# Layer boundary in an explicit order, dt weights side by side, head chains from k on, SSD in one cluster

## The chip, the cores and the metric

The kernel runs on one core of a Trainium2 chip. A core has a matrix engine (TensorE, PE in the profile), a vector engine (VectorE, DVE), an engine for pointwise functions (ScalarE, ACT), a general one (GpSimd, POOL) and an engine that here only issues transfers (SyncE, SP). Each works through its own queue of instructions in order, and semaphores hold an instruction back until what it needs is there. The metric is the device time of one execution in microseconds (us), as the median of several runs; lower is better.

## The reference

The input is one sequence of 256 frames of width 2048, ahead of which 16 learned meta tokens are set: 272 columns in the kernel (`T`). Two residual layers follow.

- Layer 0: `proj = h @ w_in` is cut into the operands of two kinds of attention, GLA (4 heads) and stick-breaking attention (8 heads of 128, operands sq, sk, sv and a gate sr). Both results, gated, are multiplied by `w_out`.
- Then `h = layer_norm(alpha * h + f)` over the 2048 features, and again behind layer 1.
- Layer 1: `z, xbc, dt = split(h @ w_in)`. `xbc` goes through a causal depthwise convolution of 4 taps and SiLU and is cut into x (8 groups of 8 heads of 64), B and C (one each per group). `dt` is one number per token and head, through softplus. The state-space scan (SSD) makes, for each head, `y[t] = sum over s <= t of exp(a[t] - a[s]) * (C[t] . B[s]) * dt[s] * x[s]` plus a skip term. y is gated by `silu(z)`, normalised per group and multiplied by a second `w_out`.

```python
for layer in range(DEPTH):          # 2
    f = even_mixer(h, ...) if layer % 2 == 0 else odd_mixer(h, ...)
    h = layer_norm(DEEPNORM_ALPHA * h + f, ln_g[layer], ln_b[layer])
return h[:, PREFIX:]                # the 256 frames
```

All of it is float32.

## The kernel before

**Products.** Activations and weights are both split into a high and a low part that TensorE takes at full rate, and a product is three matmuls: high by high, high weight by low activation, low weight by high activation (lines 165, 166, 167; `three`). The activations lie in `xhi` and `xlo` as 16 blocks of 128 features by 272 tokens (274 where two more columns carry the scale and the bias of the layer norm). 

**Weights.** They stream in as units of 1 MB (128 x 2048 values of `raw`, three buffers, SP's queue). Each unit is split in two halves: ScalarE writes the high part `whi` (line 146), VectorE the low part `wlo` = raw - whi (line 147; a few on GpSimd late in layer 1). `whi` and `wlo` have five buffers. While unit i is multiplied, `in_unit` splits unit i+1, one half ahead of each half of the matmuls, and loads unit i+2. A unit of an input projection is 48 matmuls, 24 for each half.

**Side tasks.** Everything else (heads, convolution, decay, normalisation) is written as Python generators that `tick` steps once at fixed places between matmuls. The order in which the kernel is written is not yet the order of the engines: a scheduler sorts each engine's instructions by its own estimate of when they can start, where no order is forced on it. In what follows "order" means the finished order of an engine's instructions.

**Head chains.** A stick-breaking head's chain (`mix_sb`) is pushed when its last operand v is there (`post_sv`). Its end writes `mixh` and `mixl`, which the last four units of layer 0 (`out0c`, numbers 4 to 7, the output projection of the last heads) read.

**The boundary.** Each `out0c` unit makes two blocks of 128 output features. `hacc` collects residual and output; when a block's sum is done (line 462), `stat0` writes the block's `xhi` and `xlo` (lines 815, 816: hacc scaled by the layer norm's g, not yet normalised) and adds to the sums `ssum` and `ssq` on GpSimd. `norm0` projects dt with 48 matmuls on 64 weight columns, sums `ssum` and `ssq` over the features with ones, and derives mean and 1/sigma per token, kept in two PSUM banks (`mean_p`, `rs_p`, the tiles z0 and z1 of the program). `first1` then multiplies the first six units of layer 1 (B, C, z0, x0, x1, x2) by the rows that are not yet normalised and puts mean and 1/sigma in afterwards (`fix`, lines 893 to 896). Meanwhile `normalize0` normalises `hacc` itself in 16 blocks: two steps on VectorE (lines 921, 922) and one on ScalarE (line 923). When that is through, `xhi` and `xlo` are rewritten (lines 914, 915) for the units from x3 on; `residual1` transposes `hacc` for the residual of layer 1 (lines 936, 937), and `dt_path` computes the decays. `units` goes on from the seventh unit.

**Behind a unit.** `post` takes a finished product out of PSUM: convolution (first tap on ScalarE, line 989; three more on VectorE, line 993), SiLU as Exp, Ln and Exp on ScalarE (lines 1001 to 1003). Four PSUM buffers `pj` hold products of units, two `po` all else.

**SSD.** Per group `mix_ssd` runs two clusters of fp32 matmuls for y, each for two pairs of heads (j and j+1): line 1159 (256 columns), line 1161 (144 columns), line 1163 (a corner of 16 columns on 16 rows). The two heads of a pair fill the two halves of PSUM's partitions. The operands of the corner are `mt` (16 rows, masked by C.B) and `xd2` (16 rows of dt * x). An fp32 matmul appears as two passes in the trace, each 12 matmuls of a cluster as 24 entries.

## Time and profile before

| | |
|---|---|
| runs of the kernel before | 1409.22, 1409.69, 1409.75 us; median 1409.69 |
| the profiled execution's own time | 1410.01 us |
| its span in the trace | 1408.3 us |
| granted TensorE clock, mean | 0.998 |
| matmuls / VectorE / ScalarE instructions | 10765 / 1613 / 1138 |
| last `out0c` matmul to the first matmul of x3 (the boundary) | 681.1 to 732.5 us |

The times of the steps below are those of the one profiled execution. In a timeline a row has the start, the length, the engine, the line of the code, the operation, what it writes and reads, the shape, and how many like it are put together; in brackets stands how long the engine was idle ahead of it and which instruction ended that. PE's matmuls overlap, so a matmul's length is longer than its step to the next. A group of instructions has busy time, mean length in ns, idle time of the engine ahead of it and what ended that.

### The profile page before, as it was taken

The numbers are of one execution on the slowest core, as the hardware profiler recorded it, in microseconds if no ns is written. First come the engines' busy times: TensorE is split into PE (matmuls) and PEld (weight loads), VectorE is DVE, ScalarE is ACT, GpSimd is POOL, SyncE is SP. The second block draws the span as 40 slices with busy tenths as digits, with TensorE's granted clock in tenths as the row PEclk, the third lists the DMA queues.
The fourth block names the chain that finished last, engine by engine and source line by source line (L and its number), as shares of the span: only waits on it lengthen the run. The fifth ranks groups of instructions, "written<-read, shape, count | busy, mean of one in ns | idle before, by whom it ended". The sixth has DMA issues, their size and how long they took to land.

```text
span 1408.3 us, 26132 instructions
## 1 busy us (share of the span) xinstructions
PE 1390.1 (99%) x10765; PEld 1332.7 (95%) x10765; DVE 1003.8 (71%) x1613; ACT 769.3 (55%) x1138; POOL 320.9 (23%) x285
## 2 busy tenths in 40 slices
PE   9999999999999999999999999999999999999996
PEld 8999999999999999999999999899898999989985
DVE  7857575575565675558799988776776868767587
ACT  6645454354345544555586866555555565555551
POOL 0000100100101100015301434343342432424323
PEclk9999999999999999999999999999999999999999
DMA  9544444545454445443446556555545455554551
GB/s 324 183 154 168 162 162 168 175 155 180 150 180 153 160 159 190 163 151 120 150 150 240 179 180 221 178 208 185 217 161 222 152 205 204 177 186 150 206 209 60
DMA packets 37718, 249.82 MB, mean 177 GB/s; under 512 B 4256, under 2 KB 6112, under 8 KB 9184
## 3 DMA queue, kind: packets, MB, share of 16 engines
q1 hardware_dynamic: 37168, 247.77, 50.3%
q8 instruction: 84, 1.38, 0.4%
q10 hardware_dynamic: 432, 0.39, 0.1%
q14 instruction: 34, 0.28, 0.1%
HBM read 245.94 MB, written 2.20 MB: 176 GB/s over the span
## 4 chain that ended last, share of the span: by engine, by line
PE 89%; DVE 6%; ACT 2%; issue 1%; DMA 1%; POOL 0%; ACTq 0%; SPq 0%; DVEq 0%; POOLq 0%
PE pj L165 23%; PE pj L166 23%; PE pj L167 23%; PE pj L476 4%; PE pj L478 4%; PE pj L477 4%; DVE wlo L147 2%; PE po L1159 1%; PE po L590 1%; ACT whi L146 1%; DVE xlo L816 1%; PE po L1161 1%; PE po L1163 0%; ACT hacc L923 0%; DMA ebc<-edr 0%
## 5 line engine op out<-in xcount | busy, mean ns | idle before, releaser
L165 PE MATMUL pj<-xhi,whi 128*128 128x272 f32 (+4 forms) x2560 | 734.1, 287 | 2.0 <-DVE fix L894 1.5
L166 PE MATMUL pj<-xlo,whi 128*128 128x272 f32 (+4 forms) x2560 | 731.7, 286 | 0.2 <-DVE xlo L318 0.2
L167 PE MATMUL pj<-xhi,wlo 128*128 128x272 f32 (+4 forms) x2560 | 730.3, 286 | 0.0
L147 DVE TENSOR_TENSOR wlo<-raw,whi 128x1024 fp32r<-128x1024 f32 (+2 forms) x405 | 507.0, 1256 | 254.4 <-ACT whi L146 253.1
L146 ACT ACTIVATE whi<-raw 128x1024 fp32r<-128x1024 f32 (+2 forms) x435 | 451.0, 1039 | 397.7 <-PE pj L166 335.3
L165 PEld LDWEIGHTS pj<-xhi,whi 128*128 128x128 f32 x2560 | 481.8, 188 | 4.7 <-DVE fix L894 1.9
L166 PEld LDWEIGHTS pj<-xlo,whi 128*128 128x128 f32 x2560 | 483.0, 189 | 1.8 <-issue 0.6
L167 PEld LDWEIGHTS pj<-xhi,wlo 128*128 128x128 f32 x2560 | 481.9, 188 | 0.3
L165 PE MATMUL pj<-mixh,whi 128*128 128x272 f32 x384 | 110.9, 290 | 1.0 <-ACT mixh L801 1.0
L167 PE MATMUL pj<-mixh,wlo 128*128 128x272 f32 x384 | 110.4, 288 | 0.0
L166 PE MATMUL pj<-mixl,whi 128*128 128x272 f32 x384 | 110.4, 288 | 0.0
L147 POOL TENSOR_TENSOR wlo<-raw,whi 128x1024 fp32r<-128x1024 f32 x30 | 75.4, 2513 | 132.5 <-ACT whi L146 132.4
L476 PE MATMUL pj<-whi,yh 128*128 128x512 f32 (+1 forms) x244 | 94.9, 391 | 0.0
L478 PE MATMUL pj<-whi,yl 128*128 128x512 f32 (+1 forms) x244 | 94.3, 387 | 0.0
L477 PE MATMUL pj<-wlo,yh 128*128 128x512 f32 (+1 forms) x244 | 94.2, 386 | 0.0
L248 POOL TENSOR_TENSOR gr<-gr,gsc 128x1088 f32<-128x1088 f32 x6 | 15.4, 2575 | 302.9 <-ACT gsc L247 302.9
L165 PEld LDWEIGHTS pj<-mixh,whi 128*128 128x128 f32 x384 | 72.2, 188 | 1.3 <-ACT mixh L801 1.1
L166 PEld LDWEIGHTS pj<-mixl,whi 128*128 128x128 f32 x384 | 72.3, 188 | 0.2
L167 PEld LDWEIGHTS pj<-mixh,wlo 128*128 128x128 f32 x384 | 72.3, 188 | 0.1
L485 DVE SCALAR_TENSOR_TENSOR acc<-pj,rr,acc 128x512 f32<-128x512 f32 (+1 forms) x65 | 47.2, 737 | 24.4 <-PE pj L478 24.3
L478 PEld LDWEIGHTS pj<-whi,yl 128*128 128x128 f32 x244 | 45.8, 188 | 9.2
L476 PEld LDWEIGHTS pj<-whi,yh 128*128 128x128 f32 x244 | 45.8, 188 | 9.0
(327 smaller groups left out, 1521.1 us busy)
## 6 DMA issues: line engine op xcount, KB each, us to landing
raw<-in_wts SPq DMA_DIRECT2D x212, 1024.0 KB, 4.8
ebc<-edr SPq DMA_DIRECT2D x8, 1664.0 KB, 6.5
raw<-in_wts SPq DMA_DIRECT2D x9, 256.0 KB, 6.2
hacc<-in_xT SPq DMA_DIRECT2D x7, 272.0 KB, 5.3
early<-in_wts SPq DMA_DIRECT2D x2, 512.0 KB, 6.9
lg<-in_lnr SPq DMA_DIRECT2D x1, 1024.0 KB, 4.7
lb<-in_lnr SPq DMA_DIRECT2D x1, 1024.0 KB, 4.6
out_h<-acc SPq DMA_DIRECT2D x2, 512.0 KB, 2.6
```

Of the source, the lines that this page charges most:

```text
L146: self.nc.scalar.activation(hi, src, AF.Copy)
L147: eng.tensor_tensor(lo, src, hi.bitcast(F32), op=ALU.subtract)
L165: mm(ps, whi, xhi, start=first, stop=False)
L166: mm(ps, whi, xlo, start=False, stop=False)
L167: mm(ps, wlo, xhi, start=False, stop=last)
L248: mul(c, c, e, op=ALU.mult)
L476: mm(ps, yh[:, kk, tt], hi[:, k, :], start=kk == 0, stop=False)
L477: mm(ps, yh[:, kk, tt], lo[:, k, :], start=False, stop=False)
L478: mm(ps, yl[:, kk, tt], hi[:, k, :], start=False, stop=kk == 3)
L485: self.nc.vector.scalar_tensor_tensor(a, ps, r[:, t : t + 1], a, op0=ALU.mult, op1=ALU.add)
L590: mm = lambda r, a, b, start=False, stop=False: self.nc.tensor.matmul(o[:, r], a, b, start=start, stop=stop, skip_group_check=True)
L816: vec.scalar_tensor_tensor(self.xlo[:, d, :T], x, g, self.xhi[:, d, :T].bitcast(F32), op0=ALU.mult, op1=ALU.subtract)
```

## The change

It has six parts.

1. **An explicit order.** `keep_order` ties every VectorE instruction to the one written ahead of it, and every ScalarE instruction likewise, from the start of the third `out0c` unit of the last four (number 6) to the end of `first1`. These are ties of order only, with no semaphore. What is written behind `first1` may still be put between.
2. **The normalisation in pairs.** `normalize0` takes two blocks in one VectorE step (544 columns instead of 272) and yields twice behind each pair. `first1` multiplies its first four units one after another, as before, and the last two in turns by halves, with the rewriting of `xhi` and `xlo` written in between. `residual1` and `dt_path` wait for `rows_done`.
3. **dt's weights side by side.** They are loaded and split two units earlier, high and low parts next to each other as 128 columns: two matmuls per block (by `xhi`, by `xlo`), 32 in all instead of 48. One fp32 matmul with `add2` (two identities under each other) adds the halves, after `rows_done`. The split of layer 1's second unit moves up into `norm0`.
4. **Head chains from k on.** `post_sk` pushes the chain, which waits for v only where v is used.
5. **SSD in one cluster.** The corners of the two pairs of heads of one PSUM bank become one matmul of 48 rows by 2 x 16 columns (rows 0 to 15 and 32 to 47 used, zeros else). `mt2` and `xd2` are cleared once and written by four small VectorE steps each per group. A group has one cluster of 20 matmuls, not two of 12.
6. Lines move: the three matmuls are lines 178 to 180 now, the split 159 and 160, `fix` 923 to 926, `normalize0` 983, 984 and 987, convolution 1058 and 1062, the rewriting 967 and 968, the sum into `hacc` 480, the transposes 1002 and 1003, SSD 1235 and 1241.

```diff
+    def keep_order(self, first):
+        ins = self.traced()
+        n0 = next(n for n in reversed(range(len(ins))) if ins[n] is first)
+        free = mybir.DependencyInfo(mybir.DependencyClass.NoSync, mybir.DependencyReason.DATA)
+        for eng in (mybir.EngineType.DVE, mybir.EngineType.Activation):
+            mine = [i for i in ins[n0:] if i.engine == eng]
+            for a, b in zip(mine, mine[1:]):
+                self.tc.add_manual_dep(b, a.name, free, reason="keep_order")
...
         if u[2] == 6:
-            self.dt_raw = self.lp.tile([P, 1024], F32, tag="gu", name="dtraw")
-            self.nc.sync.dma_start(self.dt_raw, self.wdt)
-        if u[2] == 7:
-            self.dt_parts = self.split(self.dt_raw, 1024)
+            self.first = self.traced()[-1]
+        if u[2] == 4:
+            self.dt_raw = self.lp.tile([P, 2, 8, 64], F32, tag="gu", name="dtraw")
+            self.nc.sync.dma_start(self.dt_raw.rearrange("p a k c -> p (a k c)"), self.wdt)
+        if u[2] == 5:
+            self.dt_parts = [self.lp.tile([P, 8, 2, 64], F32R, tag=n, name="dt" + n, bufs=2) for n in ("gvh", "gvl")]
+            for a, p in enumerate(self.dt_parts):
+                self.split_into(self.dt_raw[:, a], p[:, :, 0, :], p[:, :, 1, :], self.nc.vector)
...
     def post_sk(self, ps, h, j):
-        self.cur["k"] = self.sb_parts(ps, ("ke", "gk")[h % 2], 1.0)
+        k = self.sb_parts(ps, ("ke", "gk")[h % 2], 1.0)
+        v = self.cur["sv", h] = self.v_tiles(h)
+        self.mixers[4 + h // 4].append(self.push(self.mix_sb(h, self.cur["q"], k, v)))
...
-            self.in_kt(self.ps_dt[:64, :TG], hi[:, k, :], lo[:, k, :], k, 0, TG)
+            w = self.dt_parts[k // 8][:, k % 8].rearrange("p a c -> p (a c)")
+            mm(self.ps_dt[:, :TG], w, self.xhi[:, k, :], start=k == 0, stop=False)
+            mm(self.ps_dt[:, :TG], w, self.xlo[:, k, :], start=False, stop=k == KT - 1)
+        for h in range(2):
+            self.split_half(len(L0) + 1, h)
...
-        for n, u in enumerate(L1[:NFIRST]):
+        for n in range(NFIRST - 2):
...
+            if n == NFIRST - 3:
+                self.split_half(i + 2, 0)
...
+        for h in range(2):
+            for m, (n, ps) in enumerate(zip(ns, pss)):
+                if m == 0:
+                    self.load_unit(i + 2 + h)
+                else:
+                    self.split_half(i + 1 + h, 1 - h)
+                if (h, m) == (1, 1):
+                    self.split_half(i + 2, 1)
...
+                for k in range(8 * h, 8 * h + 8):
+                    self.in_kt(ps[:, : TG - t0], hv[:, k % 8, :], lv[:, k % 8, :], k, t0, TG)
+                    if m:
+                        act(self.xhi[:, k, :T], self.hacc[:, k, :], AF.Copy)
...
+                    if k % 4 == 3:
+                        self.tick()
+        for n, ps in zip(ns, pss):
+            self.post(L1[n], fix(ps, P, T0(n)))
+        self.rows_done = True
+        self.keep_order(self.first)
 
     def normalize0(self):
-        for k in range(KT):
-            h = self.hacc[:, k, :]
-            nc.vector.tensor_tensor(h, h, self.mean_p, op=ALU.subtract)
-            nc.vector.tensor_tensor(h, h, self.rs_p, op=ALU.mult)
-            nc.scalar.activation(h, h, AF.Identity, bias=self.col(C_LB, k), scale=self.col(C_LG, k))
-            if k % 2:
-                yield
+        two = lambda a: a.rearrange("p (o t) -> p o t", o=1).broadcast_to([P, 2, T])
+        for k in range(0, KT, 2):
+            h = self.hacc[:, k : k + 2, :]
+            nc.vector.tensor_tensor(h, h, two(self.mean_p), op=ALU.subtract)
+            nc.vector.tensor_tensor(h, h, two(self.rs_p), op=ALU.mult)
+            for kk in (k, k + 1):
+                a = self.hacc[:, kk, :]
+                nc.scalar.activation(a, a, AF.Identity, bias=self.col(C_LB, kk), scale=self.col(C_LG, kk))
+            yield
+            yield
...
+                for p, o in enumerate(os):
+                    for s, t0, c0, c1 in ((0, 0, 0, 256), (1, 112, 256, 400)):
+                        for jj in range(2):
+                            for i in range(2):
+                                h = 4 * p + 2 * jj + i
+                                mm(
+                                    o[i * 64 : (i + 1) * 64, jj, t0:S], xd[:, s, h * 64 : (h + 1) * 64], M[:, h, c0:c1],
```

Three places of the finished order show what moves. The first is VectorE at the start of layer 1. Before, from the fix of B on (`fix`, `uv`), the steps of the normalisation (L921, L922, on `hacc`) stand in blocks, with the splits (`wlo`, L147) of several units behind them:

```order
L921 TENSOR_TENSOR hacc<-hacc,z_64 128x272 x3
L894 SCALAR_TENSOR_TENSOR fix_8216<-dt_scr,uv_8215,pj_8134 128x272
L921 TENSOR_TENSOR hacc<-hacc,z_64 128x272 x8
L147 TENSOR_TENSOR wlo_8369<-raw_8226,whi_8368 128x1024
L895 TENSOR_TENSOR dt_scr<-dt_scr,z_65 64x272
L922 TENSOR_TENSOR hacc<-hacc,z_65 128x272 x8
L895 TENSOR_TENSOR fix_8216<-fix_8216,z_65 128x272
L922 TENSOR_TENSOR hacc<-hacc,z_65 128x272 x8
L893 COPY uv_8309<-pj_8228 128x2
L147 TENSOR_TENSOR wlo_8420<-raw_8319,whi_8419 128x1024
L147 TENSOR_TENSOR wlo_8460<-raw_8319,whi_8459 128x1024
L147 TENSOR_TENSOR wlo_8516<-raw_8416,whi_8515 128x1024
```

Now, from the second half of z0 on, one pair (L983, L984) stands behind each split (L160), with C's fix and convolution (`bc`) between:

```order
L160 TENSOR_TENSOR wlo_8202<-raw_8128,whi_8201 128x1024
L983 TENSOR_TENSOR hacc<-hacc,z_64 128x544
L984 TENSOR_TENSOR hacc<-hacc,z_65 128x544
L160 TENSOR_TENSOR wlo_8234<-raw_8128,whi_8233 128x1024
L983 TENSOR_TENSOR hacc<-hacc,z_64 128x544
L984 TENSOR_TENSOR hacc<-hacc,z_65 128x544
L923 COPY uv_8265<-pj_8200 128x2
L924 SCALAR_TENSOR_TENSOR fix_8266<-dt_scr,uv_8265,pj_8200 128x260
L925 TENSOR_TENSOR fix_8266<-fix_8266,z_65 128x260
L1062 SCALAR_TENSOR_TENSOR bc_8193<-fix_8266,cpk,bc_8193 128x256 x3
L160 TENSOR_TENSOR wlo_8279<-raw_8198,whi_8278 128x1024
```

The 32 steps became 16 wider ones that are spread over the splits of z0, x0, x1 and x2.

The second is ScalarE at the same place. Before, four splits (`whi`) stand ahead of the scalings of `hacc` (L923):

```order
L146 ACTIVATE whi_8368<-raw_8226 128x1024
L146 ACTIVATE whi_8419<-raw_8319 128x1024
L146 ACTIVATE whi_8459<-raw_8319 128x1024
L146 ACTIVATE whi_8515<-raw_8416 128x1024
L896 ACTIVATE dt_scr<-dt_scr,uv_8127 64x272
L923 ACTIVATE hacc<-hacc,cpk 128x272 x4
```

Now each split (L159) stands behind two scalings (L987), here from z0's second half to x0's second half, where the SiLU of B and C (L1070 to L1072) is in between:

```order
L987 ACTIVATE hacc<-hacc,cpk 128x272 x2
L159 ACTIVATE whi_8233<-raw_8128 128x1024
L987 ACTIVATE hacc<-hacc,cpk 128x272 x2
L926 ACTIVATE fix_8266<-fix_8266,uv_8265 128x260
L1058 ACTIVATE bc_8193<-fix_8266,cpk 128x256
L159 ACTIVATE whi_8278<-raw_8198 128x1024
L1003 ACTIVATE acc<-po_8671 128x512
L987 ACTIVATE hacc<-hacc,cpk 128x272 x2
L1070 ACTIVATE xcl_8298<-xcl_8298 128x528
L1071 ACTIVATE xcl_8298<-xcl_8298,b_one 128x528
L1072 ACTIVATE xcl_8298<-xcl_8298 128x528
L159 ACTIVATE whi_8316<-raw_8198 128x1024
```

The splits moved behind the scalings and fixes that are written ahead of them.

The third is TensorE in an SSD cluster of a middle group, between matmuls of the output projection. Before, one of two clusters of a group:

```order
L1159 MATMUL po_10634<-M_10120,xd_10095 64x256 x2
L1161 MATMUL po_10634<-M_10120,xd_10095 64x144 x2
L1163 MATMUL po_10634<-mt,xd_1231_10096 64x16 x2
L1159 MATMUL po_10635<-M_10120,xd_10095 64x256 x2
L1161 MATMUL po_10635<-M_10120,xd_10095 64x144 x2
L1163 MATMUL po_10635<-mt,xd_1231_10096 64x16 x2
```

Now the only one:

```order
L1235 MATMUL po_14356<-M_13783,xd_13828 64x256 x4
L1235 MATMUL po_14356<-M_13783,xd_13828 64x144 x4
L1241 MATMUL po_14356<-mt_8119,xd_8120 64x2x16 x2
L1235 MATMUL po_14357<-M_13783,xd_13828 64x256 x4
L1235 MATMUL po_14357<-M_13783,xd_13828 64x144 x4
L1241 MATMUL po_14357<-mt_8119,xd_8120 64x2x16 x2
```

A bank now holds two pairs of heads, and the corners (16 columns) halve in number.

More of the change, by code (lines that the diff above doesn't have):

```diff
@@ L149, in split_half @@
     def split_half(self, i, h):
-        if i < NU:
+        if i < NU and (i, h) not in self.parts:
             n = i - len(L0)
@@ L792, in mix_sb @@
         yield
-        yield from _wait(tv, self.tasks["sr", h // 4])
+        while ("sv", h) not in self.tasks:
+            yield
+        yield from _wait(self.tasks["sv", h], self.tasks["sr", h // 4])
         o = self.po()
@@ L901, in first1 @@
         act(mean, self.mean_p, AF.Copy)
-        self.tasks["dt"] = self.push(self.dt_path(fix(self.ps_dt, 64, 0, scr[:, 2048 : 2048 + T]), scr))
+        add2 = lp.tile([P, 64], F32, tag="add2", name="add2")
+        vec.tensor_tensor(add2, self.ident[:, :64], self.ident[:, 64:], op=ALU.add)
+        both = scr[:, 2048 + 2 * T : 2048 + 2 * T + TG]
+        act(both, self.ps_dt[:, :TG], AF.Copy)
+        self.tasks["dt"] = self.push(self.dt_path(add2, both, lambda ps: fix(ps, 64, 0, scr[:, 2048 : 2048 + T]), scr))
@@ L930, in residual1 @@
         yield from _wait(norm)
+        while not self.rows_done:
+            yield
         for t in range(2):
@@ L938, in residual1, with dt_path @@
                 yield
-    def dt_path(self, ps, scr):
+    def dt_path(self, add2, both, fix, scr):
         nc, lp = self.nc, self.lp
@@ L944, in dt_path @@
         H = 64
-        for _ in range(16):
+        while not self.rows_done:
             yield
+        pd = self.po()
+        nc.tensor.matmul(pd[:64, :TG], add2, both, start=True, stop=True)
+        ps = fix(pd)
         m, e, s, s2, p = [scr[:H, i * T : (i + 1) * T] for i in range(5)]
```

80 lines of the change are left out of this document (46 added, 34 removed).

## The prediction

> **What bounds the kernel now.** I read the page first, then a table of stretches, then the timeline of TensorE (PE) at the three places that the diff touches.
>
> ```profile
> PE 1390.1 (99%) x10765; PEld 1332.7 (95%) x10765; DVE 1003.8 (71%) x1613; ACT 769.3 (55%) x1138; POOL 320.9 (23%) x285
> 400.00:500.00 100.00, 100.00 (x818) 99.62 (x818) 55.79 (x83) 51.25 (x73) 10.23 (x19) 1.00 0.48 160
> 700.00:720.00 20.00, 20.00 (x165) 20.00 (x164) 20.00 (x49) 13.40 (x24) 0.00 (x0) 1.00 0.27 93
> 720.00:740.00 20.00, 18.25 (x145) 17.56 (x143) 19.19 (x41) 18.63 (x39) 0.00 (x0) 1.00 0.52 181
> ```
>
> (The page's line gives busy time, share and instructions of each engine; a stretch has its length, then busy time and count by engine in that order, the granted clock of PE, DMA share and GB/s.) PE is the bound: every us that it waits is a us of the kernel, and every us of matmul taken out is one gained. Undisturbed it starts 818 matmuls in 100 us, one each 0.122 us; that is the pace against which I count waits. VectorE (DVE) is idle 29% of the kernel, but at the layer boundary it is the engine without a gap (20.00 of 20, 19.19 of 20), and PE's count drops to 145 in 20 us. So the sum has three places: the last attention head and dt's projection (640 to 690), the boundary (700 to 825), and the SSD clusters of layer 1.
>
> **Step 1, the last head and dt: about -4.8 us.**
>
> ```profile
> 648.67 0.22 PE L590 MATMUL po<-s,v 80*128 80x16 f32 x1
> 649.88 0.76 PE L165 MATMUL pj<-mixh,whi 128*128 128x272 f32 x4 [0.99 <-ACT mixh L801]
> ...
> 684.99 1.21 DVE L147 TENSOR_TENSOR wlo<-raw,whi 128x1024 fp32r<-128x1024 f32 x1
> 686.12 0.77 DVE L462 TENSOR_TENSOR hacc<-hacc,pj 128x272 f32<-128x272 f32 x2
> ...
> 683.75 0.29 PE L165 MATMUL po<-xhi,whi 128*64 128x274 f32 x1
> ...
> 686.24 0.29 PE L167 MATMUL po<-xhi,wlo 128*64 128x274 f32 x1
> 687.15 0.34 PE L165 MATMUL po<-xhi,whi 128*64 128x274 f32 x1 [0.62 <-ACT xhi L815]
> 687.69 0.34 PE L166 MATMUL po<-xlo,whi 128*64 128x274 f32 x1 [0.19 <-DVE xlo L816]
> ...
> 688.84 0.34 PE L165 MATMUL po<-xhi,whi 128*64 128x274 f32 x1 [0.68 <-ACT xhi L815]
> ```
>
> PE steps from 648.67 to 649.88, 1.2 us for a step of 0.1: a wait of 1.1 us for head 7's mixed rows. The change starts each chain when k is there instead of v, and puts 28 matmuls (3.4 us) between head 7's values and their first use; 3.4 covers 1.1, so -1.1.
>
> dt: 48 matmuls become 32, at 0.125 each (683.75 to 686.24 in 20 steps): -2.0. A small fp32 matmul that adds the two halves comes in, two passes of 0.22: +0.45. In the same rows PE waits 0.79 + 0.41 + 0.84 = 2.0 us over the pace, because the last sum into hacc starts at 686.12, right behind a split that began at 684.99. In the new order the last unit's two sums and their xlo stand ahead of the splits of C, so the last xlo is there about 2 us after its matmuls, while 30 dt matmuls (3.7 us) precede its use: -2.0. What is late next there is nothing up to the statistics. dt's weights load two units earlier on SP's queue, and their two splits move with them; I price that at nothing, since the raw buffers run two units ahead of PE, and a loss would show as a wait of at most one split's 1.2 us. Together -1.1 - 2.0 + 0.45 - 2.0 = -4.65.
>
> **Step 2, the boundary: the new wait.** Before, the 32 DVE steps of the normalisation stand nearly in one block and the splits ahead of it, so PE meets its waits late:
>
> ```profile
> 729.92 0.60 PE L936 MATMUL po<-ident,hacc 128*128 128x128 f32 x4
> 731.04 0.66 PE L936 MATMUL po<-ident,hacc 128*128 128x128 f32 x4 [0.52 <-ACT acc L937]
> 732.49 0.39 PE L165 MATMUL pj<-xhi,whi 128*128 128x272 f32 x1 [0.80 <-DVE fix L894]
> ...
> 740.24 0.39 PE L165 MATMUL pj<-xhi,whi 128*128 128x256 f32 x1 [0.67 <-DVE fix L894]
> ```
>
> These are 0.68 + 0.96 + 0.83 us over the pace, and by my estimate about 1.3 more in smaller steps up to 823, half as much as in the large ones: 3.8 us, which the new order can free, as DVE then has no work left over behind x2.
>
> In the new order each half unit has a pair of 544-wide steps on DVE, two scalings of hacc on ScalarE (ACT), the split's whi on ACT and its wlo on DVE, and the next pair stands behind that wlo. Each needs the one ahead, so it is a loop:
>
> ```profile
> L147 DVE TENSOR_TENSOR wlo<-raw,whi 128x1024 fp32r<-128x1024 f32 x41 | 49.7, 1219 | 8.1 <-ACT whi L146 8.1
> L1068 DVE TENSOR_TENSOR M<-M,cb 128x800 f32<-128x800 f32 x8 | 7.6, 972 | 0.0
> L922 DVE TENSOR_TENSOR hacc<-hacc,z 128x272 f32<-128x272 f32 x16 | 5.7, 437 | 0.0
> L146 ACT ACTIVATE whi<-raw 128x1024 fp32r<-128x1024 f32 x41 | 43.1, 1053 | 21.0 <-PE pj L166 17.4 <-DMA raw<-in_wts 2.2 <-PE po L166 1.4
> L923 ACT ACTIVATE hacc<-hacc,cpk 128x272 f32<-128x272 f32 x16 | 8.7, 600 | 0.0
> L1002 ACT ACTIVATE xcl<-xcl,b_one 128x528 f32<-128x528 f32 x2 | 1.5, 732 | 0.0
> L894 DVE SCALAR_TENSOR_TENSOR fix<-dt_scr,uv,pj 128x272 f32<-128x272 f32 x4 | 2.0, 490 | 0.0
> L896 ACT ACTIVATE fix<-fix,uv 128x272 f32<-128x272 f32 x4 | 1.9, 512 | 0.0
> ...
> 789.17 1.55 DVE L993 SCALAR_TENSOR_TENSOR xt<-pj,cpk,xt 128x271 f32<-128x271 f32 x3
> ...
> 711.34 2.12 ACT L923 ACTIVATE hacc<-hacc,cpk 128x272 f32<-128x272 f32 x4
> ```
>
> A 272-wide step takes 0.437 and an 800-wide one 0.972, so a 544-wide one by the line through both is 0.71, and the dependent pair 1.45 with the hop. Two scalings are 1.11 (0.51 from start to start, 2.12 for four), whi 1.05 less an overlap of 0.09, wlo 1.22, and two hops of 0.04. The loop is 1.45 + 0.04 + 2.07 + 0.04 + 1.22 - 0.08 = **4.74 us, against PE's half unit of 24 matmuls, 2.9 to 3.1 us.** Between come the fix of the unit before (L894, L895, L896), convolution (a first ACT step, taken as L923's 0.6, and three on DVE, 1.55) and, in x0's second half, an Exp, a Ln and an Exp (0.7 each).
>
> I walked this with T the start of dt on PE.
>
> ```profile
> 694.28 0.62 PE L849 MATMUL po<-ssq,ones 128*128 128x272 f32 x2
> ...
> 699.71 0.38 ACT L901 ACTIVATE dt_scr<-z 128x272 f32<-128x272 f32 x1
> ```
>
> From the sum of squares to the rows of mean and 1/sigma it is 5.4 us here; half a us of that is a split in the way. In the new order these matmuls start at T+8.4 (dt 4.0, means 1.4, half of B 3.0), so the first pair starts at T+13.4. PE does B, C, the add and four transposes till T+19.8. Two pairs, B's fix and convolution come ahead of z0's first wlo, which ends at T+21.4.
>
> | half unit | wlo ends, T+ | PE is there, T+ | PE waits |
> |---|---|---|---|
> | z0 first | 21.4 | 19.8 | 1.6 |
> | z0 second | 26.1 | 24.5 | 1.6 |
> | x0 first (C's fix, convolution) | 32.3 | 29.2 | 3.1 |
> | x0 second (Exp, Ln, Exp) | 39.1 | 35.8 | 3.3 |
> | x1 first (z0's fix) | 44.7 | 42.4 | 2.3 |
> | x1 second | 49.4 | 47.8 | 1.6 |
> | x2 first (decay matmuls 0.8 ahead) | 54.2 | 53.4 | 0.8 |
> | x2 second (x0's fix, convolution) | 59.2 | 57.3 | 1.9 |
>
> That is +16.2. Behind x2 the next split again waits one hand-over, +0.7, and I allow +0.5 for later. Net of the 3.8 that goes: +13.6. That the last two units run in turns adds nothing: their 96 matmuls are the same, and in the instruction order x1's 48 still stand ahead of x2's; the rewriting of xhi and xlo beside them lies behind x2's last wlo, and if it were late it would be by one step of 0.5. Bounds: if every hand-over overlapped, a loop of 3.7 would leave about 1 us a half, +8; if each conv and silu step came whole, +19. I take the sum of rows.
>
> A rule stands beside this. The Trainium skill, "TensorE: Matmul & The Clock Gate", Part 1, on engine queue depths, says that ScalarE and VectorE are strict FIFO and only TensorE may pull weight loads ahead; it speaks against this change, since no split can pass a waiting normalisation step. The trace agrees: the sum into hacc at 686.12 ran only when the split of 684.99 was through.
>
> **Step 3, SSD in one cluster: -6.9 us.**
>
> ```profile
> 987.25 0.39 PE L477 MATMUL pj<-wlo,yh 128*128 128x512 f32 x1
> 987.48 0.39 PE L478 MATMUL pj<-whi,yl 128*128 128x512 f32 x1
> 987.80 0.65 PE L1159 MATMUL po<-M,xd 128*64 128x256 f32 x4
> 988.28 0.42 PE L1161 MATMUL po<-M,xd 128*64 128x144 f32 x4
> 988.63 0.29 PE L1163 MATMUL po<-mt,xd 16*64 16x16 f32 x4
> 988.85 0.65 PE L1159 MATMUL po<-M,xd 128*64 128x256 f32 x4
> ...
> 989.89 0.50 PE L476 MATMUL pj<-whi,yh 128*128 128x512 f32 x1
> 990.23 0.39 PE L477 MATMUL pj<-wlo,yh 128*128 128x512 f32 x1
> ...
> 988.07 0.39 PE L1159 MATMUL po<-M,xd 128*64 128x256 f32 x2
> 988.40 0.29 PE L1161 MATMUL po<-M,xd 128*64 128x144 f32 x2
> ```
>
> Half a cluster takes 1.05 us: 0.48 for the 256-wide, 0.35 for the 144-wide, 0.22 for the 16-wide. Going in costs 0.09 (0.32 against 0.23), coming out 0.11 (0.34 against 0.23). In a run of one shape the first pair takes 0.27 and a further one 0.21 (988.07 to 988.28), or 0.12 at 144 (988.28 to 988.40), 0.23 ahead of the change of shape. The new half has four pairs, four pairs and one short block: 0.27 + 3 x 0.21 + 3 x 0.12 + 0.23 + 0.22 = 1.71 instead of 2.09. A group has two such halves and one entry and exit less: -0.76 - 0.2, about -0.93 with the rounding; seven groups -6.5, and group 0, in fragments by other work, -0.4. Bounds: were each pair of heads to pay its start again, 1.88, so -0.6 a group and -4.7; none at all saved, 0; at best -7.5. The six more small DVE writes a group lie beside PE, where DVE is idle later; without that cover they would cost about 1 us a group.
>
> **The sum.** The profiled execution took 1410.01 us (span 1408.3, 1.7 around it), 0.3 above the median of 1409.69. 1410.0 - 4.65 + 13.6 - 6.9 = 1412.0, and 0.3 less against the median: 1411.7. Within 0.2% is 1406.9 to 1412.5, about what a measurement of this kernel can tell from no change.
>
> **Rivals.**
> - *Faster: the loop is half hidden.* For: rows at ACT and DVE overlap by 0.1, and the block of 32 steps is half as many instructions. Against: every link is a true dependence. With +8 instead of +16 it is 1403.5; with none of it, 1395.
> - *Slower: the cluster saves nothing.* The saving is a sum of spacings inside 1 us. If the changes of tile shape (128 rows to 16, now to 48) set the time and not the count of matmuls, step 3 falls to about -1.5 and the time is 1417. It decides from a saving below 6.1 us on. For it: 0.23 instead of 0.12 at the change of shape. Against: the further pairs do run at 0.21 and 0.12.
> - *Slower by the clock.* With PE idle some 2 us in each 5, the granted clock might fall.
>
> ```profile
> 1402.00:1404.00 2.00, 0.00 (x0) 0.00 (x0) 1.97 (x2) 0.00 (x0) 1.60 (x1) 0.50 0.48 193
> ```
>
>   Where PE had nothing for several us the clock was 0.50; in the boundary of before it was 1.00. At half clock a half unit takes 6 us, more than the loop, and two or three of them add 6 us: 1418. The same page, Part 1, puts the idle window at about 3.4 us; my longest wait is 3.3, so by that rule it would be a near thing; no row here shows a wait of that length in mid-kernel.
> - *It doesn't do what it says:* the scheduler undoes the order. Excluded by the instruction order, in which the rows stand so.
>
> **Chances.** Forecast as summed (1406 to 1415) 0.56, of it within 0.2% 0.34; loop half hidden or better 0.27; cluster without saving 0.11; clock 0.06. Faster by over 0.2%: 0.28; within: 0.35; slower: 0.37. The range of 8 in 10 reaches into both sides, 1400.5 to 1418.
>
> **What would show it.** Right: eight waits of PE for DVE's wlo (L160) of 1 to 3 us, from dt's end on; x2 ending 62 us after dt's start; the wait for mixh, and those for xhi in dt, gone; an SSD cluster of 3.4 us instead of two of 2.1. Wrong: waits in the eight half units under 8 us in all, PE waiting for something other than wlo there (transposes, buffers of pj), a cluster over 3.9 us, or a clock under 1.00 before the tail.

## The result and the profile after

The changed kernel takes **1427.3 us** (median of four runs, 1426.5 to 1427.8), the kernel before 1409.7. The ratio is 1.0124 with a 95% interval of 1.0112 to 1.0137: 17.6 us slower. 1411.7 was forecast, with a chance of 0.35 for a change within 0.2% and of 0.37 for a slower kernel, and the range ended at 1418. One of the four runs of e6 (an experiment below) took 4335.7 us; its time and ratio in the table are those of the other three.

The page of the changed kernel, PE's line and the two groups that wait:

```profile
PE 1388.8 (97%) x10687; PEld 1333.6 (94%) x10687; DVE 1029.2 (72%) x1649; ACT 771.1 (54%) x1140; POOL 315.2 (22%) x285
...
L178 PE MATMUL pj<-xhi,whi 128*128 128x272 f32 (+4 forms) x2560 | 735.7, 288 | 14.7 <-ACT gz L1203 11.1
L180 PE MATMUL pj<-xhi,wlo 128*128 128x272 f32 (+4 forms) x2560 | 733.4, 287 | 7.4 <-DVE wlo L160 7.4
```

PE has 78 matmuls fewer and is busy for a shorter time than before, but its share fell from 99% to 97%: more waiting, not more work. The two rows name the waits. 7.4 us ahead of `wlo` matmuls, and 3.0 more ahead of `whi` matmuls, are the loop of the prediction. 11.1 us ahead of a `whi` matmul, released by ScalarE's copy of `gz`, are in no part of it. The stretches show where (columns as before):

```profile
700.00:720.00 20.00, 13.29 (x83) 11.71 (x83) 12.64 (x19) 10.04 (x16) 1.31 (x1) 0.91 0.15 53
720.00:740.00 20.00, 16.32 (x105) 14.76 (x105) 12.14 (x21) 12.35 (x23) 0.71 (x3) 0.92 0.30 105
740.00:760.00 20.00, 19.69 (x165) 19.44 (x165) 19.52 (x34) 14.51 (x24) 0.00 (x0) 1.00 0.75 262
...
820.00:840.00 20.00, 14.95 (x131) 12.96 (x129) 19.79 (x42) 11.40 (x19) 7.15 (x7) 0.98 0.74 276
840.00:860.00 20.00, 13.92 (x112) 12.72 (x113) 13.93 (x32) 9.38 (x21) 6.53 (x8) 0.76 0.31 106
```

From 700 to 740 PE has 188 matmuls, where the two stretches of before have 310, and VectorE, which was full there before, is busy for 24.8 of 40 us. It makes up for that from 740 on (19.5 of 20). From 820 to 860 PE loses a second stretch.

To place the difference I count matmuls of units and compare the moment of the same one in both traces. At the last `out0c` units the changed kernel is 1.4 us ahead (0.4 of it from the start of the kernel), at C's first matmul 5.7 ahead, six units behind dt, where x3 begins, **10.2 behind**, 1020 unit matmuls further (875.8 us before) **21.3 behind**, and at the last unit of the input projection 17.3 behind.

**The loop.** PE's timeline in the boundary, six of the thirteen rows with a wait, and then one turn of the loop on VectorE and ScalarE:

```profile
701.51 0.39 PE L180 MATMUL pj<-xhi,wlo 128*128 128x258 f32 x1 [1.28 <-DVE wlo L160]
706.26 0.39 PE L180 MATMUL pj<-xhi,wlo 128*128 128x258 f32 x1 [0.76 <-DVE wlo L160]
710.82 0.39 PE L178 MATMUL pj<-xhi,whi 128*128 128x274 f32 x1 [1.44 <-ACT whi L159]
712.56 0.40 PE L180 MATMUL pj<-xhi,wlo 128*128 128x274 f32 x1 [1.23 <-DVE wlo L160]
719.55 0.41 PE L180 MATMUL pj<-xhi,wlo 128*128 128x274 f32 x1 [1.01 <-DVE wlo L160]
739.75 0.40 PE L180 MATMUL pj<-xhi,wlo 128*128 128x274 f32 x1 [1.27 <-DVE wlo L160]
...
701.37 0.71 DVE L983 TENSOR_TENSOR hacc<-hacc,z 128x544 f32<-128x544 f32 x1
702.12 0.72 DVE L984 TENSOR_TENSOR hacc<-hacc,z 128x544 f32<-128x544 f32 x1
702.88 1.12 ACT L987 ACTIVATE hacc<-hacc,cpk 128x272 f32<-128x272 f32 x2 [2.47 <-DVE hacc L984]
703.90 1.04 ACT L159 ACTIVATE whi<-raw 128x1024 fp32r<-128x1024 f32 x1
704.98 1.23 DVE L160 TENSOR_TENSOR wlo<-raw,whi 128x1024 fp32r<-128x1024 f32 x1 [2.14 <-ACT whi L159]
706.12 0.71 DVE L983 TENSOR_TENSOR hacc<-hacc,z 128x544 f32<-128x544 f32 x1
```

From one L983 to the next it is 706.12 - 701.37 = 4.75 us. While ScalarE scales and writes `whi`, VectorE waits 2.14 us; while VectorE does the pair, ScalarE waits 2.47. Neither is full, and neither can go on.

**The long wait.** PE, GpSimd, VectorE and ScalarE in order of cause:

```profile
834.67 0.28 PE L180 MATMUL pj<-xhi,wlo 128*128 128x256 f32 x1
846.08 0.59 PE L178 MATMUL pj<-xhi,whi 128*128 128x272 f32 x1 [11.14 <-ACT gz L1203]
...
837.01 0.51 ACT L1248 ACTIVATE yh<-yu,cpk 128x256 fp32r<-128x256 f32 x1 [1.68 <-POOL yu L1246]
838.41 1.11 DVE L1137 TENSOR_TENSOR M<-M,cb 128x800 f32<-128x800 f32 x1
841.18 0.88 DVE L1249 SCALAR_TENSOR_TENSOR yl<-yu,cpk,yh 128x256 fp32r<-128x256 f32 x2
...
843.32 0.85 DVE L1245 SCALAR_TENSOR_TENSOR yu<-xt,cpk,po 128x256 f32<-128x256 f32 x2
...
843.92 1.41 POOL L1246 TENSOR_TENSOR yu<-yu,gz 128x256 f32<-128x256 f32 x2 [5.25 <-DVE yu L1245]
...
844.75 0.31 ACT L1119 ACTIVATE mt<-mt 16x128 f32<-16x128 f32 x1 [5.99 <-DVE mt L1118]
...
845.67 1.15 ACT L1203 ACTIVATE gz<-pj 128x256 f32<-128x256 f32 x4
```

Four finished z products of group 1 fill the four `pj` buffers. Their copies (`gz`, x4) run at 845.67, all at once, after GpSimd has multiplied group 0's last y by group 0's z (843.92 and on), because the z tile has one buffer; on ScalarE they also stand behind `mt`, which is later than they need. Group 0's y is late: its clusters run at 819 to 828, and at 784 to 794 before. VectorE has hardly a gap in the wait (busy for 9.9 us from 834 to 844): ScalarE is through with group 0's second y (`yh`) at 837.5, but VectorE's part of the first two (`yl`) stands behind group 1's decay (`M`), and the next two y (`yu`, two buffers) come behind that. Up to 3.7 of the 11 us may lie in that order; no run changed it alone.

**SSD.** One cluster of a middle group:

```profile
1088.18 0.39 PE L496 MATMUL pj<-whi,yl 128*128 128x512 f32 x1
1088.49 1.57 PE L1235 MATMUL po<-M,xd 128*64 128x256 f32 x16
1090.00 0.30 PE L1241 MATMUL po<-mt,xd 48*64 48x32 f32 x4
1090.23 1.57 PE L1235 MATMUL po<-M,xd 128*64 128x256 f32 x16
1091.74 0.30 PE L1241 MATMUL po<-mt,xd 48*64 48x32 f32 x4
1091.97 0.50 PE L494 MATMUL pj<-whi,yh 128*128 128x512 f32 x1
```

1088.49 to 1091.97 is 3.48 us, for two clusters of 2.09 before: 0.70 less, and with one entry and one exit less (0.09 and 0.11 in the rows of before) 0.9 a group. A row that puts shapes together shows the first one's: the x16 are eight entries of 256 columns and eight of 144.

### The profile page after: what moved, and what is told of

It reads as the page before. It is cut to its first block, busy times and chain, and to the rows that moved or that the text cites. A ratio compares the mean times of both kernels' runs of the same rounds, so it can differ in the third digit from the quotient of the medians.

```text
span 1424.8 us, 26024 instructions
## 1 busy us (share of the span) xinstructions
PE 1388.8 (97%) x10687; PEld 1333.6 (94%) x10687; DVE 1029.2 (72%) x1649; ACT 771.1 (54%) x1140; POOL 315.2 (22%) x285
## 5 line engine op out<-in xcount | busy, mean ns | idle before, releaser
L178 PE MATMUL pj<-xhi,whi 128*128 128x272 f32 (+4 forms) x2560 | 735.7, 288 | 14.7 <-ACT gz L1203 11.1
L160 DVE TENSOR_TENSOR wlo<-raw,whi 128x1024 fp32r<-128x1024 f32 (+2 forms) x405 | 511.4, 1267 | 265.8 <-ACT whi L159 264.2
L159 ACT ACTIVATE whi<-raw 128x1024 fp32r<-128x1024 f32 (+2 forms) x435 | 450.5, 1038 | 393.3 <-PE pj L179 324.1
L160 POOL TENSOR_TENSOR wlo<-raw,whi 128x1024 fp32r<-128x1024 f32 x30 | 75.0, 2500 | 112.7 <-ACT whi L159 112.4
```

Source lines behind the costliest of these rows:

```text
L159: self.nc.scalar.activation(hi, src, AF.Copy)
L160: eng.tensor_tensor(lo, src, hi.bitcast(F32), op=ALU.subtract)
L178: mm(ps, whi, xhi, start=first, stop=False)
```

## The experiments

The numbers in the table: median and ratio to the kernel before on the same chip, how many us the kernel is behind the kernel before (+) or ahead of it (-) six units behind dt (288 matmuls; x3 begins there), and 1020 unit matmuls further on. These last two are read from the one profiled execution of each kernel, which lies up to 2.0 us from the median (e3: 1405.0 and 1407.0).

| run | median us | ratio, 95% interval | six units on | 1020 more |
|---|---|---|---|---|
| the changed kernel | 1427.3 | 1.0112 to 1.0137 | +10.2 | +21.3 |
| e1 scalings two ticks later | 1422.6 | 1.0070 to 1.0100 | +4.8 | +16.1 |
| e2 two z buffers | 1426.8 | 1.0096 to 1.0129 | +9.9 | +21.3 |
| e3 old boundary, three parts | 1407.0 | 0.9963 to 0.9985 | -2.9 | -0.5 |
| e4 no forced order | 1411.0 | 0.9994 to 1.0012 | -5.0 | +5.4 |
| e5 forced, dt and residual free | 1432.6 | 1.0149 to 1.0183 | +26.2 | +25.8 |
| e6 e3 with the order up to norm0 | 1402.0 | 0.9928 to 0.9962 | -5.6 | -3.5 |
| e7 order up to norm0, both free | 1403.9 | 0.9941 to 0.9971 | -7.8 | -0.5 |
| e8 SSD alone | 1406.2 | 0.9961 to 0.9983 | +0.7 | +0.7 |
| e9 splits half a unit earlier | 1430.5 | 1.0133 to 1.0167 | +11.7 | +23.9 |
| e10 order up to norm0, held | 1405.9 | 0.9965 to 0.9983 | -9.8 | +0.2 |
| e11 e7, pairs one tick apart | 1400.4 | 0.9919 to 0.9949 | -7.9 | -7.2 |
| e12 forced, dt alone free | 1427.3 | 1.0109 to 1.0140 | +24.2 | +22.3 |

Theories: **L**, the boundary's waits are the loop; **Z**, the long wait comes from dt_path being held to `rows_done`, by way of z's single buffer; **D**, it is VectorE's work put off by the loop; **C**, the lower clock and not the waits costs the boundary. From the second set on, **R** is Z without the z buffer: the chain from dt_path to group 1 begins too late.

**e1, the scalings behind the next whi.**

```diff
             nc.vector.tensor_tensor(h, h, two(self.rs_p), op=ALU.mult)
+            yield
+            yield
             for kk in (k, k + 1):
                 a = self.hacc[:, kk, :]
                 nc.scalar.activation(a, a, AF.Identity, bias=self.col(C_LB, kk), scale=self.col(C_LG, kk))
-            yield
-            yield
```

> The changed kernel, but each pair's two ScalarE scalings are written two ticks later, behind the next split's whi instead of ahead of it; the VectorE order is unchanged. Theory L (the boundary's waits are the loop pair, scalings, whi, wlo, next pair): the loop is cut where nothing else is due; I walk the queues again and get PE waits of 1.4, 0, 2.7, 2.8, 2.2, 0, 0, 1.3 in the eight half units, 10 instead of 13 to 16, and x2 ending 6 us earlier, about T+57 after dt's start instead of T+63. Theory Z (the 11.1 us wait at 834.67 comes from dt_path being held to rows_done and the single z buffer): that wait keeps its place behind x2 and its length within 3 us, so the time is about 1421. Rival D (the 11.1 us wait is VectorE work put off by the idle time in the loop): VectorE gains some 6 us, so the wait shrinks to 5 or less and the time is about 1414. Rival C (the lower clock, not the waits, costs the boundary): x2 ends within 1 us of before this edit unless the clock of 700:740 rises to 1.00.

With T the start of dt on PE, x2 ends, and x3 begins, at T+57.0 instead of T+62.9: 5.9 us less by moving sixteen instructions in ScalarE's queue. The long wait stayed:

```profile
840.91 0.60 PE L178 MATMUL pj<-xhi,whi 128*128 128x272 f32 x1 [11.11 <-ACT gz L1203]
```

11.11 us after 11.14: what VectorE gained in the loop did nothing to it. That speaks against D; L held in size. The granted clock of 700 to 740 rose only from 0.91 to 0.96, not to 1.00, so C doesn't explain the 5.9 us.

**e2, a second buffer for z.**

```diff
-            self.cur["z", g] = self.lp.tile([P, 4, S], F32, tag="gz", name=self.nm("gz"))
+            self.cur["z", g] = self.lp.tile([P, 4, S], mybir.dt.bfloat16, tag="gz", name=self.nm("gz"), bufs=2)
```

> The changed kernel, but the gate tile z of layer 1 has two buffers, kept in bfloat16 so that both fit (z and its gate are rounded to bfloat16, so the output differs in its low digits). Boundary untouched: x2 must again end about T+63. Theory Z: group 1's z products can leave the four pj buffers while group 0's y is still unfinished, so the 11.1 us wait on the copy of z goes, with the cold clock behind it: 1427 - 11 to 13 = about 1415. Rival D (VectorE's backlog): z's copy no longer waits, but PE then stops as long for another piece of late VectorE work (wlo, cluster operands): 1423 to 1427.

A miss for Z as I had put it: 1426.8 lies in the range that D gave, and e4 and e12 have to tell D from R. The 11 us are gone from `gz`, and PE waits elsewhere for the same late groups:

```profile
854.23 1.23 PE L1261 MATMUL po<-ones,ysq 128*128 128x128 f32 x4 [2.90 <-POOL ysq L1255]
...
895.54 1.11 PE L1174 MATMUL po<-ident,xt 128*128 128x128 f32 x4 [3.73 <-POOL xt L1073]
```

Both stand for y and x of groups that came late, and 1020 matmuls on it is again 21.3 behind. The single buffer is only where the lateness first reached PE.

**e3, the old boundary with three parts** (chains from k on, dt side by side, one SSD cluster; `first1`, `normalize0`, `residual1`, `dt_path` and their order as before; dt's halves are added at once).

```diff
-        self.rows_done = True
-        self.keep_order(self.first)
...
+        pd = self.po()
+        nc.tensor.matmul(pd[:64, :TG], add2, both, start=True, stop=True)
+        self.tasks["dt"] = self.push(self.dt_path(fix(pd, 64, 0, scr[:, 2048 : 2048 + T]), scr))
```

> The kernel before with three of the six parts: head chains from k on, dt's weights side by side and loaded and split early (the halves added at once), and SSD in one cluster. first1, normalize0, residual1 and dt_path are as before, without the forced order. If the summed prices hold alone: -1.1 (head) - 3.6 (dt) - 6.3 (SSD as the trace of the changed kernel shows it, 0.9 a group) = 1398.7, range 1396 to 1402. If the gain of SSD or dt hangs on the new boundary, 1403 or more. If the free scheduler answers to the moved pieces with new waits at the boundary, over 1405, and the waits stand at 700 to 830.

1407.0 lies over the bounds of both "if not" cases, and the waits show both. dt's gain did hang on the order, since PE waits in dt as it did before; and new waits stand at the boundary, 4.1 us at x3 and behind it, where it was 1.5:

```profile
684.99 0.40 PE L853 MATMUL po<-xhi,dtgvl 128*128 128x274 f32 x1 [1.65 <-ACT xhi L822]
...
729.63 0.36 PE L165 MATMUL pj<-xhi,whi 128*128 128x272 f32 x1 [2.18 <-ACT xhi L932]
739.54 0.39 PE L165 MATMUL pj<-xhi,whi 128*128 128x256 f32 x1 [1.97 <-DVE fix L906]
```

**e4, the changed kernel without the forced order.**

```diff
         self.rows_done = True
-        self.keep_order(self.first)
```

> The changed kernel without the call that forces the order; all else stays, the pairs, the last two units in turns and dt_path behind rows_done. Theory L with the forced order as its cause: the scheduler puts splits ahead of scalings again, PE waits in the eight half units fall from 13 to under 5 us, x2 ends by T+52. Theory Z: dt_path still starts only behind x2, so a wait of several us on the copy of z stays: about 1414 to 1419. Rival D: with VectorE busy through the boundary no long wait is left: about 1403.

Left to the scheduler, the boundary has no loop. PE's stretch there, and its two waits behind x3:

```profile
700.00:740.00 40.00, 40.00 (x324) 39.44 (x323) 38.12 (x75) 33.24 (x60) 1.33 (x1) 1.00 0.49 168
```

```profile
825.85 0.60 PE L1177 MATMUL z<-ident,xt 128*16 128x128 f32 x2 [4.82 <-POOL xt L1072]
829.61 0.60 PE L178 MATMUL pj<-xhi,whi 128*128 128x272 f32 x1 [3.16 <-ACT gz L1202]
```

324 matmuls in 40 us for 188, and x3 at T+47.0 for T+62.9, although e4 waits in dt again (1.6 us for `xhi`). Counted from C's first matmul to x3, which leaves dt out, **the loop's price is 20.2 us**, and it is the forced order that makes it, not the pairs or the turns, which are still there. 1411.0 lies between what Z and D gave. VectorE is full in the boundary (38.1 of 40), so no work is put off by a loop, yet 8 us of waits stay behind x3, for x and z of group 1. D, as it was put, is out.

**e5, dt_path and the residual not held, order kept.**

```diff
-        while not self.rows_done:
+        for _ in range(16):
             yield
...
         yield from _wait(norm)
-        while not self.rows_done:
-            yield
```

> The changed kernel with the forced order kept, but dt_path (after 16 ticks) and residual1 (behind the normalisation) no longer wait for rows_done, as in the kernel before. Theory L: the loop is untouched, so the boundary's waits stay and grow by up to 5 us, since dt_path's VectorE steps now stand in the forced queue: x3 starts 10 to 15 us later than before the change. Theory R (the long wait at 834.67 is the chain dt_path, decay of group 0, SSD of group 0, decay and SSD of group 1, begun too late because it is held to rows_done): group 0's cluster comes some 250 matmuls earlier and the long wait goes: 1427 - 12 + 0 to 5 = 1415 to 1420. Rival D (VectorE's backlog from the loop): a wait of 8 us or more stays behind x3: 1424 or more.

The time is not the 1415 to 1420 that R gave, but R's mechanism held: group 0's first cluster comes 239 unit matmuls earlier, and behind x3 nothing is lost (+26.2 at x3, +25.8 further on). My bound for the boundary was wrong: not up to 5 but 16 us more. dt_path's chain in the forced queue makes PE wait for its rows in the middle of x2.

**e6, e3 with the order from the `out0c` units to the end of `norm0` only.**

```diff
+        self.keep_order(self.first)
         self.first1()
```

> As the run with the old boundary (chains from k on, dt side by side, SSD in one cluster), with the forced order added from the third last-but-one out0c unit to the end of norm0 only. If dt's own saving needs the order (its matmuls waited 1.9 + 0.4 us there for xlo of the last block): these waits go and B starts 2 us or more earlier, 1407.0 - 2.3 = about 1404.5. If they are moved and not removed: 1407 as without.

1402.0, 5.0 us less than e3 where 2.3 were expected: PE no longer waits in dt, and at C's first matmul it is 6.2 us ahead of the kernel before instead of 3.5. Its largest wait is now the one at x3, for `xhi` of the normalised rows:

```profile
726.91 0.56 PE L178 MATMUL pj<-xhi,whi 128*128 128x272 f32 x1 [2.17 <-ACT xhi L946]
```

**e7, the new boundary with the short order, both not held** (the edits of e5 and e6 on the changed kernel).

> The changed kernel with the forced order only up to the end of norm0, and dt_path and residual1 not held to rows_done; pairs and the last two units in turns stay. Theory L and theory R together: no loop (-15), no long wait (-9 to -12): 1398 to 1403, with x3 starting 5 us or more earlier than in the kernel before. If the long wait is SSD's single cluster rather than the late chain, a wait of 5 us or more stays at 800 to 840 and the time is 1405 or more.

1403.9, just above the range. The boundary is faster than in every run above it, and then PE gives most of it back, waiting for x and z of group 1 (2.9 and 2.2 us at 814 to 822). My reading is that with pairs two ticks apart the residual is written 8 ticks later, and group 0's decay waits for it; e11 tests that.

**e8, SSD in one cluster alone**, on the kernel before.

```diff
-            if j % 2 == 0:
-                os = {jj: self.po() for jj in (j, j + 1)}
+            if j == 0:
+                os = [self.po() for _ in range(2)]
```

> The kernel before with SSD in one cluster of 20 matmuls as its only edit. By the prediction's sum 6.9 us less, by the slope of the changed kernel's trace (0.8 a group from the third group on) about 6: 1404. Rival: the single cluster holds both po buffers at once, and what waits for po pays the gain back: 1408 to 1410, with new waits of PE for po or yu in each group.

1406.2, 3.5 us less. Groups 0 and 1, which are packed with late work, brought nothing (+0.7 at x3 and +0.7 further on). The next five bring 3.7 us by the last unit of the input projection: 0.9 at each cluster, as the rows above say, less some 0.3 us that PE now waits ahead of a transpose of x in three of them. The profile names x (GpSimd) for these waits; that it is `po`, as the rival has it, is not shown. The +0.7 at x3 comes from dt: PE waited in dt as it did in the kernel before, but here the clock fell behind these waits (688.56), and 1.4 us went.

**e9, each split of `first1` written half a unit earlier.**

```diff
-            self.in_unit(ps[:, : TG - t0], i, t0, TG, lambda h: self.split_half(i + 1, h))
+            self.in_unit(ps[:, : TG - t0], i, t0, TG, lambda h: self.split_half(i + 1 + h, 1 - h))
```

> The changed kernel with each split of first1 written half a unit earlier, under the same forced order. Theory L: the loop sets the rate, so a head start of half a unit is used up after the first wait; walking the queues again gives PE waits of 0 for z0's first half and then 1.8, 1.7, 3.3, 3.7, 2.5, 1.0, 3.7, and x2 ending at T+62 to 63 as before the edit; time 1426 to 1428. Rival (the splits are only written too late by a fixed amount, and would be in time with half a unit more): the waits go, x2 ends by T+50 and the time falls by 10 us or more, to 1417 or less.

x3 at T+64.6 and 1430.5, some 2 us past what I walked: nothing is gained, and the rival's 1417 is out. A head start is used up at once where a loop sets the rate.

**e10, the short order, dt_path and residual held.**

```diff
+        self.keep_order(self.first)
         self.rows_done = False
         self.first1()
...
         self.rows_done = True
-        self.keep_order(self.first)
```

> The changed kernel with the forced order only up to the end of norm0; dt_path and residual1 stay held to rows_done. Against the run without any forced order (1411.0) the order up to norm0 should bring dt's part, about 4: 1407. Against the run that is the same but not held (1403.9) this prices the holding where no loop is: theory R gives a wait of about 8 us on z's copy behind x2 and 3 us more in all: 1407. Rival D (the late chain matters only behind a loop): no difference to 1403.9.

This differs from the changed kernel only in how far the order reaches: **1405.9 for 1427.3, so 21.4 us are the forced order inside `first1`.** x3 comes 20 us earlier. The long wait is there too, 6.95 us:

```profile
824.21 0.59 PE L178 MATMUL pj<-xhi,whi 128*128 128x272 f32 x1 [6.95 <-ACT gz L1203]
```

Against e7 holding saves 2.0 us ahead of x3 and loses 2.7 more behind it; the medians differ by 2.0, and their intervals overlap, so that what holding costs in all without the loop is not shown.

**e11, e7 with one tick between pairs.**

```diff
                 nc.scalar.activation(a, a, AF.Identity, bias=self.col(C_LB, kk), scale=self.col(C_LG, kk))
             yield
-            yield
```

> The changed kernel with the forced order only up to the end of norm0, dt_path and residual1 not held, and the pairs one tick apart instead of two, so that the residual and with it the decay of group 0 can begin some 8 ticks earlier. In the run with two ticks (1403.9) PE waited 2.9 + 2.2 us at 814 to 822 for work of groups 0 and 1. Theory R: the earlier chain takes most of these waits away: 1399 to 1401. If VectorE is full there anyway (19.3 of 20 at 800:820) the waits move: 1403 to 1405.

1400.4, 0.66% under the kernel before and 1.9% under the changed one, the best of these. The waits at 814 to 822 fall to one of 1.6, at the same place, and the clock, which fell to 0.50 there in e7, stays at 1.00:

```profile
817.71 0.40 PE L178 MATMUL pj<-xhi,whi 128*128 128x272 f32 x1 [1.59 <-ACT gz L1200]
```

Its interval (0.9919 to 0.9949) overlaps that of e6 (0.9928 to 0.9962), so that the new boundary beats the old one with the same three parts is not shown.

**e12, order kept, dt_path alone not held** (the first of e5's two edits).

> The changed kernel, forced order kept, with only dt_path not held (16 ticks), residual1 still behind rows_done. In the run with both free the long wait of 11 us went and the boundary cost 16 us more, of which dt's transposes waiting on VectorE took 5 and the residual's transposes about 5. If both costs are dt_path's steps in the forced queue: x3 starts 20 us or more later than in the kernel before. If the long wait hangs on dt_path and not on the residual it is gone: 1427 - 12 + 10 to 15 = 1425 to 1430. If it hangs on the residual (the decay of group 0 waits for both), it stays: 1435 or more.

The long wait is gone (+24.2 at x3, +22.3 further on) although the residual is still held: it hangs on dt_path. SSD's single cluster is in this run too, so the wait is not the cluster's. And the time is that of the changed kernel, 1427.3: around x2 PE pays what it saves later, here waiting for splits that stand behind dt_path's steps:

```profile
742.81 0.60 PE L178 MATMUL pj<-xhi,whi 128*128 128x274 f32 x1 [4.48 <-ACT whi L159]
746.32 0.59 PE L178 MATMUL pj<-xhi,whi 128*128 128x272 f32 x1 [2.68 <-ACT whi L159]
```

## Why the prediction was wrong

**Step 1, head and dt: right.** -1.0 at the head (-1.1 forecast) and -4.3 from there to C (-4.0, the add comes later). e3 and e4 add what the prediction had only from the order: without it dt waits 1.65 us again. (The step's heading says -4.8, its terms and the total -4.65.)

**Step 2, the loop: right in its pace and its net, not in every sign.** Loop 4.75 us (4.74). PE's first `wlo` matmul of the eight half units stood at T+21.8, 26.5, 32.8, 39.8, 45.5, 50.2, 55.0, 60.0 (T = 679.74), each 0.4 to 0.8 us behind the `wlo` ends of the forecast's table. Against no loop the price is 20.2 us (e4, e10), not 16.2: the forecast's own walk without waits was too slow, about T+46 at x3 (62 less 16.2), where e10 has T+42.7. Against the kernel before, 15.8 us went from C to x3, and the forecast's terms up to there make about 15. PE's idle time in the loop is 10.4 us in thirteen waits of 0.2 to 1.4, eight of them for `wlo` (0.4 to 1.3), so the sign "eight waits of 1 to 3 us" came in number and not in size. e9 shows that it is a rate and not a delay, e1 that ScalarE's side of it can be cut.

**Step 2, "I allow +0.5 for later", and "DVE then has no work left over behind x2": this failed.** It put the cost behind x3 at next to nothing, +0.7 and +0.5 less some 2 that the new order would free there; 11.2 us were lost in the 1020 unit matmuls from x3 on. VectorE was busy 19.5 of 20 us behind x2, with dt_path and the decays, and PE lost 11.1 us at 834.67 and about 1.7 more at half clock behind that: 19 matmuls started from 846 to 850, where 33 would have at 0.122 us each. That is 12.8 of the 15.6 us by which the forecast was short. I had the instruction order, in which group 0's clusters stand some 190 matmuls later; I did not ask who waits for them. They free z's buffer, and z's copies free `pj`. The change holds dt_path to `rows_done` and so takes it out of the forced queue, where it costs 14 to 16 us (e5, e12), and pays 11 behind x3. Within the forced order holding dt_path is a trade of equals (e12, 1427.3 both ways); the order itself is the loss (e10).

**Step 3, SSD: the mechanism right, the sum too large.** 3.48 us a cluster (3.42), so 0.92 a group. Of 6.9 us 3.5 arrived in e8: groups 0 and 1 give nothing, about 0.3 us comes back in three others, and 1.4 us went in dt, where the clock fell. In the changed kernel the last six groups bring it from 21.3 behind to the 16.5 by which the two profiled executions differ. The rival by which shapes set the time is out: the pairs kept 0.21 and 0.12.

**The clock: the rival came true in part.** It fell in the boundary and in the long wait. In the boundary that cost little, since the loop set the pace, not PE: behind both cold spells PE still waited for the next split (0.66 and 1.01 us at 718 to 720, 0.64 at 725.24). Behind the long wait it cost the 1.7 us above.

"Slower" had the most chance by a little, and slower it is; but the forecast's 2 us came from the loop less the savings, and what took the time out of the range is the wait behind x3, which no rival named.

What stays open: whether e11's boundary is better than the old one in e6; and why the long wait in e1, e9 and the changed kernel is 11.1 us each time while x3 moves by 7. That fits a chain that starts at `rows_done` and moves along with PE's own place, but no run took that chain apart.

## What to carry to other kernels

An order forced on two engines at once ties every handover between them into one chain: sum the chain through both queues for one turn and compare it with what the engine they feed needs in that time, since neither's busy share shows it. Force an order only over the stretch where it is wanted (here up to `norm0`: 21 us less). When a side chain is put off, follow its outputs to the buffers they free, and count who stops when these stay full.

## What the runs showed of the hardware

The granted clock of PE fell sooner than I thought. In the changed kernel's boundary no idle time of PE was over 1.5 us, and in e6 a single wait of 2.17 us (the row at 726.91) was enough. The stretches of the changed kernel, then those of e6:

```profile
710.00:712.00 2.00, 0.52 (x2) 0.30 (x2) 1.93 (x4) 1.24 (x2) 0.00 (x0) 1.00 0.13 53
714.00:716.00 2.00, 2.00 (x10) 2.00 (x10) 0.24 (x1) 1.97 (x4) 0.00 (x0) 0.50 0.04 8
...
846.00:848.00 2.00, 1.92 (x8) 1.92 (x9) 1.22 (x3) 2.00 (x8) 0.97 (x2) 0.50 0.00 0
848.00:850.00 2.00, 2.00 (x13) 2.00 (x12) 0.00 (x0) 2.00 (x5) 0.41 (x1) 0.62 0.00 0
```

```profile
726.00:728.00 2.00, 1.09 (x5) 1.12 (x6) 2.00 (x7) 2.00 (x7) 0.00 (x0) 0.72 0.02 4
728.00:730.00 2.00, 2.00 (x11) 2.00 (x11) 2.00 (x6) 2.00 (x6) 0.00 (x0) 0.50 0.48 70
730.00:732.00 2.00, 2.00 (x17) 2.00 (x17) 2.00 (x7) 1.63 (x4) 0.00 (x0) 0.92 0.72 299
```

At 0.50 a stretch of 2 us holds 10 or 11 matmuls, for 19 at full clock. In e6 the wait cost 2.2 us, and the cold spell some 1.5 more (15 matmuls at 0.23 us instead of 0.12).

The cold spells of the boundary and of e6 lasted 3.41 us each (from 712.97, 719.80 and 726.89), the one at the long wait 10.24, three times that. So I cut each trace into steps of 3.41 us that fall in with its own cold spells. Ahead of the two falls in the boundary PE was idle for 2.48 and 1.67 us of the step, ahead of that in e6 for 2.15. Over all fourteen traces every step at full clock with 1.84 us or more of idle time was followed by 0.50, and none with 1.44 or less; between the two (1.45 to 1.75) both happened. So the sum of idle time in a step counts, and where the steps lie decides too: the same waits in dt make 1.05 us of one step in the kernel before, which kept its clock, and 1.51 in e8, which lost it. The Trainium skill, "TensorE: Matmul & The Clock Gate", Part 1, gives a free-running window of about 3.4 us, and a whole idle window for the clock to fall. The length of the steps agrees with that, but the wait had not to be that long.
